# A two-layer encoder on one core: one of two dense blocks finished behind the next layer's first normalisations, with 90 instead of 50 late gather steps

## The chip, the cores and the metric

The kernel runs on one core of a Trainium2 chip. The metric is the time of one execution in microseconds (us) as the device measures it; lower is better. The engines of the core are named as the profile names them: PE (TensorE, matrix products), PEld (its weight loads), DVE (VectorE), ACT (ScalarE), POOL (GpSimd, which also issues the gathers) and SP (SyncE, which issues the ordinary loads). Each engine takes its instructions in the order in which they stand in its queue.

## The reference

The input is 512 tokens of width 1024, with two layers. Each layer mixes tokens and then applies a lookup layer named PEER, each with a residual and a normalisation:

```
h   = LN(x) * (1 + scale1(c)) + shift1(c)
mix = W_o [ MLA(h) | ShortConv(h) | StickBreaking(h) ]
x   = LayerNorm(alpha * x + (1 + gate1(c)) * mix)
h   = LN(x) * (1 + scale2(c)) + shift2(c)
x   = LayerNorm(alpha * x + (1 + gate2(c)) * PEER(h))
```

PEER has 128 x 128 experts, each with one row of a table u and one row of a table v (1024 floats each). A token has 8 heads with 16 chosen experts each, so 128 experts. For each of them the output gets gelu(u_e . h) times the expert's weight times v_e. The choice is made by queries against two sets of 128 keys and two rounds of top-k.

## The kernel before

The 512 tokens are four blocks of 128 (NB = 4), blocks 0 to 3. In a layer every block passes prepare (a normalisation, the tile `ytok`, and its transposes `hT`), project (the input projection, done for blocks 0 and 1 together and for 2 and 3 together), attend, output, between (residual, normalisations, `h2d`), queries and the top-k (topk, which ends with the integer indices `eidx`).

PEER is computed in two ways. Blocks 1 and 2 (DENSE) go through dense(): for each of the 128 key rows the whole rows of u and v are loaded (512 KB each), the scores of all 256 tokens are made (L824 to L826), Gelu (L828), times the gate weights G (L830), and summed into `acc` in PSUM (L854 to L860). G is built in three parts, for rows 0 to 51, 52 to 75 and 76 to 127 (CUTS); the part for rows 52 to 75 is built during rows 0 to 51, the last during rows 52 to 75. Blocks 0 and 3 go through experts(): 256 gather steps a block, each an indirect DMA of one row a token (issued by POOL, L689 for u, L701 for v) into one of four buffers `g`, and one DVE operation on it, a dot (L691) for u or a sum into `acc` (L706) for v, in groups of 32 dots, Gelu (L695) and 32 sums. So a layer has 512 steps.

pace() lays the steps among the rest: EARLY (80 in layer 0, 110 in layer 1) before the dense rows, 32 during the first build, LATE[l] behind the dense rows, and the remaining ones evenly over the 128 rows. A step is tied to a mark: its DVE operation may not come before the marked one. The order on each engine is then made by a scheduler that knows priorities; finish() of a gathered block has a higher priority than all else. In layer 0 the late steps are the last ones of block 3.

finish() adds the gate row, the residual and the last normalisation of a block (L223, L718, L237, L239, L225) and writes `xs[b]`, which the next layer's prepare(b) reads. After the last dense row, dense() copies both blocks' sums from PSUM into two tiles `fa` and finishes both, with tiles from the dense pass's own pools (`dw`, `dps`), which are given back by st.close() afterwards. The mark of the late steps is the finish of block 1. The next layer opens its attention pools, lays the 50 late steps, and goes on with layer_setup (SP's loads of small tables, L287 and on), prepare, layer_keys and project (weights by L151, matmuls L154). Block 3's finish and prepare(3) need all late steps.

Of the kernel before, what the change touches and what calls it, by code (L numbers as in the profile page):

```python
# [11 lines left out]
F32 = mybir.dt.float32  # L12
# [5 lines left out]
OP = mybir.AluOpType  # L18
# [3 lines left out]
P = 128  # L22
D = 1024
# [10 lines left out]
CUTS = (0, 52, 76, 128)  # L34
DENSE = (1, 2)
EARLY = (80, 110)
LATE = (50, 0)
WK = 2
HB = 2
MG = 4  # L40
# [12 lines left out]
def body(ctx, tc, x, c, positions, ada_w, ada_b, w_in, q_norm_g, kv_norm_g, w_uq, w_ukv, conv_w,  # L53
         w_o, ln1_g, ln1_b, peer_wq, peer_k1, peer_k2, peer_u, peer_v, ln2_g, ln2_b, out):
    nc = tc.nc
# [4 lines left out]
    pw = ctx.enter_context(tc.tile_pool(name="pw", bufs=1))  # L60
# [59 lines left out]
    rest = 2 * math.pi  # L120
# [122 lines left out]

    def normalize(dst, src):
        mean, r = moments(src)
        nc.vector.tensor_scalar(dst, src, mean, r, op0=OP.subtract, op1=OP.mult)

    def affine(y, dst, tmp, src, ig, ib, mk=None, pool=None):
        mean, r = moments(src, pool)
# [101 lines left out]
    def prepare(y, b):  # L351
        hT = A.work.tile([P, KT, P], F32, name="hT", bufs=2)
        yt = A.work.tile([P, D], F32, name="ytok", bufs=1)
        normalize(yt, xs[b])
        transpose_cols(hT, yt, KT, scale=y.sc1, bias=y.sh1)
        y.hT[b] = hT

    def project(y, blocks, behind=None):
        l = y.l
# [313 lines left out]
    def experts(y, b, eidx, gw):  # L673
        def after(inst):
            if gate[0] is not None:
                tc.add_manual_dep(inst.ins, gate[0].ins.name,
                                  mybir.DependencyInfo(mybir.DependencyClass.NoSync, mybir.DependencyReason.DATA),
                                  reason="expert sums in pace with the dense tiles")

        h2 = pw.tile([P, D], F32, name="h2")  # L680
        nc.sync.dma_start(h2, h2tok[y.l][b // 2])
        acc = pw.tile([P, D], F32, name="acc")
        dots = pw.tile([P, PH, TOPK], F32, name="dots", bufs=1)
        wts = pw.tile([P, PH, TOPK], F32, name="wts", bufs=1)
        for h0 in range(0, PH, HB):
            slots = [(h, k) for h in range(h0, h0 + HB) for k in range(TOPK)]
            for j, (h, k) in enumerate(slots):
                g = gath.tile([P, D], F32, name="g")
                nc.gpsimd.indirect_dma_start(out=g, out_offset=None, in_=u_flat,  # L689
                                             in_offset=bass.IndirectOffsetOnAxis(ap=eidx[:, h, k:k + 1], axis=0))  # L690
                after(nc.vector.scalar_tensor_tensor(out=g, in0=g, scalar=1.0, in1=h2, op0=OP.mult, op1=OP.mult,  # L691
                                                     accum_out=dots[:, h, k:k + 1]))
                yield
            hs = slice(h0, h0 + HB)
            ge = nc.scalar.activation(wts[:, hs, :], dots[:, hs, :], AF.Gelu)  # L695
            if b == 0 and h0 < 2:
                exp_ln(ge)
            nc.vector.tensor_tensor(wts[:, hs, :], wts[:, hs, :], gw[:, hs, :], op=OP.mult)
            for j, (h, k) in enumerate(slots):
                g = gath.tile([P, D], F32, name="g")  # L700
                nc.gpsimd.indirect_dma_start(out=g, out_offset=None, in_=v_flat,  # L701
                                             in_offset=bass.IndirectOffsetOnAxis(ap=eidx[:, h, k:k + 1], axis=0))
                if h == 0 and k == 0:
                    r = nc.vector.tensor_scalar(acc, g, wts[:, h, k:k + 1], None, op0=OP.mult)
                else:
                    r = nc.vector.scalar_tensor_tensor(out=acc, in0=g, scalar=wts[:, h, k:k + 1], in1=acc,  # L706
                                                       op0=OP.mult, op1=OP.add)
                after(r)
                if h < PH - 1 or k < TOPK - 1:
                    yield  # L710
        tc.cur_priority -= 1000000
        finish(y, b, acc, lambda: psx.tile([P, 512], F32, name="prow", tag="ex"), pw)
        tc.cur_priority += 1000000
        yield
# [9 lines left out]
    def dense(y, blocks, res):  # L724
        l = y.l
# [165 lines left out]
                yield held[0]  # L891
        fas = []
        for i in range(2):
            fa = dw.tile([P, D], F32, name="fa", tag="v", bufs=2)
            for g in range(2):
                nc.scalar.copy(fa[:, g * 512:(g + 1) * 512], acc[i][g])
            fas.append(fa)
        for b, fa in zip(blocks, fas):
            r = finish(y, b, fa, ut, dw)
            if b == min(blocks):  # L900
                held[0] = r
        st.close()
        yield held[0]

    def pace(ex, mark, n):
        gate[0] = mark
        for _ in range(n):
            next(ex)

    ada_first(range(4))  # L910
    for l in range(L):
        if l:
            open_attention(l)
            late()
        y = layer_setup(l)

        def pick(b, v1, fi):
            return topk(l, v1, fi, b, b not in DENSE)

        res = [None] * NB  # L920
        for b in (0, 1):
            prepare(y, b)
        layer_keys(y)
        ps = project(y, (0, 1))
        if l + 1 < L:
            ada_side(0, range(4, 12))
        layer_rows(y)
        behind = None
        for p in ps:
            b = p[0]  # L930
            attend(y, *p)
            if b == 1:
                for b2 in (2, 3):
                    prepare(y, b2)
            h = between(y, b, output(y, b, p[2]))
            r = queries(y, *h, range(4))
            if b == 0:
                behind = r
            res[b] = pick(b, *h[1:])
        p2, p3 = project(y, (2, 3), behind)  # L940
        if l + 1 < L:
            ada_side(1, range(12))
        attend(y, *p2)
        h = between(y, 2, output(y, 2, p2[2]))
        queries(y, *h, range(2))
        attend(y, *p3)
        rt = output(y, 3, p3[2])
        queries(y, *h, range(2, 4))
        res[2] = pick(2, *h[1:])
        h = between(y, 3, rt, lambda: A.ps.tile([P, 512], F32, name="prow", tag="at", bufs=2))  # L950
        queries(y, *h, range(4))
        res[3] = partial(pick, 3, *h[1:])
        A.stack.close()
        dn = dense(y, DENSE, res)
        ex = chain.from_iterable(experts(y, b, *res[b]) for b in range(NB) if b not in DENSE)
        pace(ex, None, EARLY[l])
        groups = 2 * P // TG
        for _ in range(groups):
            mark = next(dn)
            pace(ex, mark, 1)  # L960
        with tc.issue_after(mark.ins):
            res[3] = res[3]()
        n = 2 * 2 * NSLOT - EARLY[l] - LATE[l] - groups
        for a, mark in enumerate(dn):
            if a < NK:
                pace(ex, mark, (a + 1) * n // NK - a * n // NK)
        late = partial(pace, ex, mark, LATE[l])
        if not l + 1 < L:
            late()


_INS = ["x", "c", "positions", "ada_w", "ada_b", "w_in", "q_norm_g", "kv_norm_g", "w_uq", "w_ukv", "conv_w",
# [19 lines left out]
```

## Time and profile before

| | before |
|---|---|
| median of 3 runs | 3501.09 us (3497.18 to 3502.11) |
| profiled execution | 3500.46 us, span 3498.7 us |
| PE busy | 3023.7 us, 86% |
| DVE busy | 2871.1 us, 82% |
| POOL busy | 1443.6 us, 41% |
| ACT busy | 1049.6 us, 30% |
| DMA | 1012.04 MB, mean 289 GB/s |

The program's course, in us from the start of the span: layer 0's attention until about 692, its dense rows until 1741, the boundary of the layers until 1797, layer 1's attention until about 2404, its dense rows until about 3451, and a tail to 3498.7. The busy shares are means over these stages, which have different limits, so each stage is read by itself: by windows (busy time of each engine in a stretch), timelines (instructions in order, in brackets the idle time before one and what ended it) and the chain of work that ended last.

### The profile page before, as it was taken

How to read it: one execution, taken by the hardware profiler on the slowest of the kernel's cores; microseconds unless marked ns; L12 is line 12 of the kernel's file. 1: busy time of each engine (PE TensorE's matmuls, PEld its weight loads, DVE VectorE, ACT ScalarE, POOL GpSimd, SP SyncE). 2: the span in 40 equal slices, each digit the busy share in tenths (PEclk: the TensorE clock that was granted, in tenths of full speed). 3: DMA queues.
4: the chain of work that ended last, by engine and by line, in shares of the span. 5: the costliest groups of instructions: out<-in, count | busy, mean ns of one | idle time of the engine just before them, and what ended most of it. 6: DMA issues, size and time to landing. Idle time of an engine off the chain costs nothing.

```text
span 3498.7 us, 52847 instructions
## 1 busy us (share of the span) xinstructions
PE 3023.7 (86%) x18708; PEld 2088.1 (60%) x18708; DVE 2871.1 (82%) x6385; ACT 1049.6 (30%) x2031; POOL 1443.6 (41%) x1347
## 2 busy tenths in 40 slices
PE   7878878658999999999948888884699999899995
PEld 2333434436777777777624444433477777777774
DVE  3567897999888998777775579889998899987777
ACT  2242433222232333322222323312223323332221
POOL 1034554255444434434451044534444444444434
PEclk9989979859999999999969997896699999999997
DMA  8667978568999888999985587794789998999997
GB/s 290 217 219 240 349 223 301 176 185 268 337 337 345 314 296 307 363 349 343 321 305 196 172 276 270 266 329 157 229 290 358 342 348 312 323 338 349 342 347 242
DMA packets 340057, 1012.04 MB, mean 289 GB/s; under 512 B 40505, under 2 KB 53065, under 8 KB 339793
## 3 DMA queue, kind: packets, MB, share of 16 engines
q0 software_dynamic: 147456, 536.94, 44.0%
q1 hardware_dynamic: 192336, 471.73, 38.5%
q8 instruction: 148, 2.42, 0.3%
q14 instruction: 117, 0.95, 0.1%
HBM read 1002.06 MB, written 6.34 MB: 288 GB/s over the span
## 4 chain that ended last, share of the span: by engine, by line
PE 49%; DVE 23%; DMA 14%; issue 8%; POOL 3%; ACT 2%; SPq 0%; POOLq 0%; DVEq 0%; ACTq 0%
PE acc L860 12%; PE pm L154 7%; PE sp L826 5%; PE sp L824 5%; PE sp L825 5%; PE utp L810 5%; DMA g<-in_peer_u,eidx 4%; DVE g L691 3%; DMA g<-in_peer_v,eidx 3%; DVE acc L706 3%; DMA adw<-in_ada_w 3%; DVE tk_ef L661 2%; DVE o L790 2%; POOL g L689 2%; PE acc L856 2%
## 5 line engine op out<-in xcount | busy, mean ns | idle before, releaser
L701 POOL DMA_INDIRECT g<-in_peer_v,eidx x512 | 616.5, 1204 | 795.9 <-DVE acc L706 522.1
L689 POOL DMA_INDIRECT g<-in_peer_u,eidx x512 | 581.2, 1135 | 740.7 <-DVE g L691 510.1
L706 DVE SCALAR_TENSOR_TENSOR acc<-g,wts,acc 128x1024 f32<-128x1024 f32 x508 | 667.3, 1314 | 73.5 <-DMA g<-in_peer_v,eidx 69.6
L691 DVE SCALAR_TENSOR_TENSOR g<-g,h 128x1024 f32<-128x1024 f32 x512 | 622.8, 1226 | 98.3 <-DMA g<-in_peer_u,eidx 96.2
L824 PE MATMUL sp<-hh,uh 128*128 128x256 f32 x2048 | 622.7, 304 | 12.9 <-ACT ge L828 11.5
L860 PE MATMUL acc<-v,ge 128*128 128x512 f32 x1360 | 619.5, 597 | 7.9 <-DVE ge L830 7.9
L826 PE MATMUL sp<-hh,ul 128*128 128x256 f32 x2048 | 596.3, 291 | 0.4 <-DVE ul L814 0.2
L825 PE MATMUL sp<-hl,uh 128*128 128x256 f32 x2048 | 588.7, 287 | 0.0
L812 ACT CAST uh<-utp 128x512 fp32r<-128x512 f32 x512 | 298.5, 590 | 694.8 <-PE utp L810 559.9
L814 DVE TENSOR_TENSOR ul<-utp,uh 128x512 fp32r<-128x512 f32 x512 | 345.6, 686 | 84.2 <-ACT uh L812 64.0
L824 PEld LDWEIGHTS sp<-hh,uh 128*128 128x128 f32 x2048 | 393.8, 192 | 31.9 <-ACT ge L828 15.9
L825 PEld LDWEIGHTS sp<-hl,uh 128*128 128x128 f32 x2048 | 393.7, 192 | 14.6 <-issue 13.2
L860 PEld LDWEIGHTS acc<-v,ge 128*128 128x128 f32 x1360 | 247.4, 191 | 251.5 <-issue 242.5
L826 PEld LDWEIGHTS sp<-hh,ul 128*128 128x128 f32 x2048 | 393.3, 192 | 0.5 <-DVE ul L814 0.4
L810 PE MATMUL utp<-ident,u 128*128 128x128 f32 x2048 | 304.9, 277 | 13.9 <-DVE ul L814 12.5
L797 PE MATMUL pg<-o,o 128*128 128x52 bf16 (+1 forms) x4608 | 189.7, 192 | 102.5 <-DVE o L790 79.3
L799 ACT COPY G<-pg 128x416 f32<-128x416 f32 (+1 forms) x192 | 146.4, 773 | 433.9 <-PE pg L797 395.8
L810 PEld LDWEIGHTS utp<-ident,u 128*128 128x128 f32 x2048 | 239.4, 142 | 61.7 <-issue 33.7
L797 PEld LDWEIGHTS <-o 128*128 128x128 bf16 x4608 | 164.5, 103 | 157.1 <-issue 79.1
L154 PE MATMUL pm<-wt,hT 128*128 128x512 f32 (+1 forms) x512 | 231.7, 601 | 30.7 <-DMA wt<-in_w_in 18.8
L154 PE MATMUL pm<-wt,h2T 128*128 128x512 f32 x512 | 234.5, 604 | 10.0 <-DMA wt<-in_peer_wq 9.6
L660 POOL TENSOR_TENSOR tk_pick<-tk_hot,tk_ce 128x400 f32<-128x400 bf16 x128 | 121.9, 953 | 145.0 <-DVE tk_hot L658 142.5
(244 smaller groups left out, 4101.2 us busy)
## 6 DMA issues: line engine op xcount, KB each, us to landing
u<-in_peer_u SPq DMA_DIRECT2D x256, 512.0 KB
v<-in_peer_v SPq DMA_DIRECT2D x256, 512.0 KB
wt<-in_peer_wq SPq DMA_DIRECT2D x128, 512.0 KB
adw<-in_ada_w SPq DMA_DIRECT2D x160, 256.0 KB
wt<-in_w_o SPq DMA_DIRECT2D x64, 512.0 KB
wt<-in_w_in SPq DMA_DIRECT2D x48, 512.0 KB
wt<-in_ada_w SPq DMA_DIRECT2D x16, 512.0 KB
g<-in_peer_u,eidx POOLq DMA_INDIRECT x512
```

The lines of the kernel that those rows point to most:

```text
L154: r = nc.tensor.matmul(pm[:, :n], lhsT=lhsT[:, k0 + k, :], rhs=wt[:, k, :n], start=k0 + k == 0, stop=k0 + k == KT - 1)
L689: nc.gpsimd.indirect_dma_start(out=g, out_offset=None, in_=u_flat, in_offset=bass.IndirectOffsetOnAxis(ap=eidx[:, h, k:k + 1], axis=0))
L691: after(nc.vector.scalar_tensor_tensor(out=g, in0=g, scalar=1.0, in1=h2, op0=OP.mult, op1=OP.mult, accum_out=dots[:, h, k:k + 1]))
L701: nc.gpsimd.indirect_dma_start(out=g, out_offset=None, in_=v_flat, in_offset=bass.IndirectOffsetOnAxis(ap=eidx[:, h, k:k + 1], axis=0))
L706: r = nc.vector.scalar_tensor_tensor(out=acc, in0=g, scalar=wts[:, h, k:k + 1], in1=acc, op0=OP.mult, op1=OP.add)
L797: nc.tensor.matmul(pg[:, tt, 0:n], lhsT=o2[:, tt // TI, :, tt % TI], rhs=o1a[:, tt // TI, p, 0:n, tt % TI], start=tt == 0 and p == 0, stop ...
L810: nc.tensor.transpose(pt[:, j * P:(j + 1) * P], u[:, k * P:(k + 1) * P], ident)
L814: nc.vector.tensor_tensor(ul.rearrange("p j t -> p (j t)"), pt, uh.rearrange("p j t -> p (j t)").bitcast(F32), op=OP.subtract)
L824: nc.tensor.matmul(sp, lhsT=uh[:, j, :], rhs=hh[:, k, :], start=k == 0, stop=False)
L825: nc.tensor.matmul(sp, lhsT=uh[:, j, :], rhs=hl[:, k, :], start=False, stop=False)
L826: nc.tensor.matmul(sp, lhsT=ul[:, j, :], rhs=hh[:, k, :], start=False, stop=k == KT - 1)
L860: nc.tensor.matmul(acc[i][g], lhsT=w[:, i * P:(i + 1) * P], rhs=v[:, g * 512:(g + 1) * 512], start=a == 0, stop=a == NK - 1)
```

## The change

After the dense rows only block 1 is finished in the dense pass. Block 2's sums are copied into a buffer of the gather pool (tag "g") instead of the dense pool, and its finish, now with the tile `prow` that the gathered blocks use (one buffer), is put in a list `rest`. In layer 1 it is issued behind prepare(0) and prepare(1); then come the late steps, 90 instead of 50, tied to prepare(1)'s normalisation instead of block 1's finish. The other steps of layer 0 become 310 instead of 350 over the 128 rows. At the end of layer 1, which has no late steps, the finish in `rest` is issued last.

```diff
-LATE = (50, 0)
+LATE = (90, 0)
...
     def normalize(dst, src):
         mean, r = moments(src)
-        nc.vector.tensor_scalar(dst, src, mean, r, op0=OP.subtract, op1=OP.mult)
+        return nc.vector.tensor_scalar(dst, src, mean, r, op0=OP.subtract, op1=OP.mult)
...
-                g = gath.tile([P, D], F32, name="g")
+                g = gath.tile([P, D], F32, name="g", tag="g")
...
-            fa = dw.tile([P, D], F32, name="fa", tag="v", bufs=2)
+            if i:
+                fa = gath.tile([P, D], F32, name="fa", tag="g")
+            else:
+                fa = dw.tile([P, D], F32, name="fa", tag="v", bufs=2)
...
-        for b, fa in zip(blocks, fas):
-            r = finish(y, b, fa, ut, dw)
-            if b == min(blocks):
-                held[0] = r
+        held[0] = finish(y, blocks[0], fas[0], ut, dw)
+        rest.append(lambda: finish(y, blocks[1], fas[1], lambda: psx.tile([P, 512], F32, name="prow", tag="ex"), pw))
         st.close()
         yield held[0]
+
+    rest = []
...
         if l:
             open_attention(l)
-            late()
         y = layer_setup(l)
...
         for b in (0, 1):
-            prepare(y, b)
+            r = prepare(y, b)
+        if l:
+            rest.pop()()
+            pace(ex, r, LATE[l - 1])
         layer_keys(y)
...
-        late = partial(pace, ex, mark, LATE[l])
         if not l + 1 < L:
-            late()
+            pace(ex, mark, LATE[l])
+            rest.pop()()
```

(prepare returns what normalize returns.) Three places show what moves on DVE. A row names the line, the operation, what it writes and reads, and how many stand in a row. `xs_95` to `xs_98` are blocks 0 to 3. The changed file's lines are one higher here (L692 for L691, L707 for L706, L719 for L718).

At the boundary of the layers, before: from block 1's residual to the statistics of block 2's finish.

```order
L718 SCALAR_TENSOR_TENSOR fa<-xs_96,fa 128x1024
L691 SCALAR_TENSOR_TENSOR g,dots<-g,h_10955 128x1024 x2
L237 BN_STATS bnst<-fa 128x6 x2
L239 BN_AGGR bnmv<-bnst 128x2
L225 SCALAR_TENSOR_TENSOR fa<-fa,bnmv,utp 128x512 x2
L225 SCALAR_TENSOR_TENSOR xs_96<-fa,rs_r,utp 128x512 x2
L691 SCALAR_TENSOR_TENSOR g,dots<-g,h_10955 128x1024 x4
L223 TENSOR_TENSOR fa<-fa,utp 128x512 x2
L691 SCALAR_TENSOR_TENSOR g,dots<-g,h_10955 128x1024
L718 SCALAR_TENSOR_TENSOR fa<-xs_97,fa 128x1024
L691 SCALAR_TENSOR_TENSOR g,dots<-g,h_10955 128x1024 x2
```

Now the same place, from the last gate row:

```order
L223 TENSOR_TENSOR fa<-fa,utp 128x512
L223 TENSOR_TENSOR fa<-fa,prow 128x512
L719 SCALAR_TENSOR_TENSOR fa<-xs_96,fa 128x1024
L719 SCALAR_TENSOR_TENSOR fa<-xs_97,fa 128x1024
L237 BN_STATS bnst<-fa 128x6 x4
L239 BN_AGGR bnmv<-bnst 128x2 x2
L225 SCALAR_TENSOR_TENSOR fa<-fa,bnmv,utp 128x512 x2
L225 SCALAR_TENSOR_TENSOR fa<-fa,bnmv,prow 128x512
L225 SCALAR_TENSOR_TENSOR xs_96<-fa,rs_r,utp 128x512 x2
L225 SCALAR_TENSOR_TENSOR fa<-fa,bnmv,prow 128x512
L298 MEMSET sqT 128x1024
```

The dots are gone from between the pieces, and the two finishes go piece by piece in turn.

In layer 1's attention, where block 0's top-k begins, before: the last stick-breaking operation and the first round.

```order
L539 SCALAR_TENSOR_TENSOR sp_18407<-z,sbe 128x512
L610 MAX tk_v<-scs 128x8 x4
L612 MAX_INDEX tk_i<-tk_v,scs 128x8 x4
L615 MATCH_REPLACE scs<-tk_v,scs 128x128 x4
L610 MAX tk_v<-scs 128x8 x4
L612 MAX_INDEX tk_i<-tk_v,scs 128x8 x4
```

Now:

```order
L540 SCALAR_TENSOR_TENSOR sp_18407<-z,sbe 128x512
L707 SCALAR_TENSOR_TENSOR acc<-g,wts,acc 128x1024 x2
L611 MAX tk_v<-scs 128x8 x4
L613 MAX_INDEX tk_i<-tk_v,scs 128x8 x4
L616 MATCH_REPLACE scs<-tk_v,scs 128x128 x3
L707 SCALAR_TENSOR_TENSOR acc<-g,wts,acc 128x1024
L616 MATCH_REPLACE scs<-tk_v,scs 128x128
L611 MAX tk_v<-scs 128x8 x4
L613 MAX_INDEX tk_i<-tk_v,scs 128x8 x4
L707 SCALAR_TENSOR_TENSOR acc<-g,wts,acc 128x1024
```

Sums of the late steps stand between the pieces of the top-k, where there were none.

At the end of the program, before: the rest of block 2's finish among sums, then block 3's (`xs_98`).

```order
L239 BN_AGGR bnmv<-bnst 128x2
L706 SCALAR_TENSOR_TENSOR acc<-g,wts,acc 128x1024
L225 SCALAR_TENSOR_TENSOR fa<-fa,bnmv,utp 128x512 x2
L706 SCALAR_TENSOR_TENSOR acc<-g,wts,acc 128x1024
L225 SCALAR_TENSOR_TENSOR xs_97<-fa,rs_r,utp 128x512 x2
L706 SCALAR_TENSOR_TENSOR acc<-g,wts,acc 128x1024 x2
L223 TENSOR_TENSOR acc<-acc,prow 128x512 x2
L718 SCALAR_TENSOR_TENSOR acc<-xs_98,acc 128x1024
L237 BN_STATS bnst<-acc 128x6 x2
L239 BN_AGGR bnmv<-bnst 128x2
L225 SCALAR_TENSOR_TENSOR acc<-acc,bnmv,prow 128x512 x2
```

Now:

```order
L225 SCALAR_TENSOR_TENSOR xs_96<-fa,rs_r,utp 128x512 x2
L707 SCALAR_TENSOR_TENSOR acc<-g,wts,acc 128x1024 x7
L223 TENSOR_TENSOR acc<-acc,prow 128x512 x2
L719 SCALAR_TENSOR_TENSOR acc<-xs_98,acc 128x1024
L237 BN_STATS bnst<-acc 128x6 x2
L239 BN_AGGR bnmv<-bnst 128x2
L225 SCALAR_TENSOR_TENSOR acc<-acc,bnmv,prow 128x512 x2
L225 SCALAR_TENSOR_TENSOR xs_98<-acc,rs_r,prow 128x512 x2
L223 TENSOR_TENSOR fa<-fa,prow 128x512 x2
L719 SCALAR_TENSOR_TENSOR fa<-xs_97,fa 128x1024
L237 BN_STATS bnst<-fa 128x6 x2
```

Seven sums stand in a row behind block 1's finish; then comes block 3's finish, and block 2's (`xs_97`) behind it.

On ACT the order holds 27 table loads (ACT_TABLE_LOAD) instead of 17. The ten new ones are all in layer 1's attention, around the stick-breaking heads (L536, L537, L549, L551) and the late steps' Gelu (L695).

## Rows read from the trace of the kernel before

**Rows 1.** Windows of dense rows: start:end, length, busy us by engine, PE clock, DMA share, GB/s

```profile
809.60:1178.10 368.50, 357.76 (x2705) 282.36 (x2704) 321.75 (x553) 107.60 (x207) 173.30 (x149) 1.00 0.91 327
1178.10:1381.70 203.60, 196.88 (x1780) 156.14 (x1779) 185.85 (x350) 73.72 (x123) 84.44 (x68) 0.99 0.86 301
1381.70:1733.20 351.50, 350.95 (x2095) 277.12 (x2096) 272.75 (x396) 100.12 (x187) 148.31 (x135) 1.00 0.95 346
...
2885.50:3094.10 208.60, 198.22 (x1766) 157.71 (x1765) 191.62 (x351) 74.03 (x124) 90.95 (x76) 0.98 0.89 314
```

**Rows 2.** The same windows, DVE's dots (L691), then its sums (L706), rows 52 to 75

```profile
1178.10:1381.70 203.60, 38.45 (x64) 0.99 0.86 301
...
1178.10:1381.70 203.60, 39.99 (x32) 0.99 0.86 301
```

**Rows 3.** Timeline of DVE at the boundary: start, us, instruction, idle before it and its releaser

```profile
1748.55 1.23 DVE L691 SCALAR_TENSOR_TENSOR g<-g,h 128x1024 f32<-128x1024 f32 x1 [1.19 <-DMA g<-in_peer_u,eidx]
...
1752.82 1.41 DVE L225 SCALAR_TENSOR_TENSOR xs<-fa,rs_r,utp 128x512 f32<-128x512 f32 x2
...
1774.70 1.23 DVE L691 SCALAR_TENSOR_TENSOR g<-g,h 128x1024 f32<-128x1024 f32 x1 [0.77 <-DMA g<-in_peer_u,eidx]
...
1775.85 1.40 DVE L225 SCALAR_TENSOR_TENSOR xs<-fa,rs_r,utp 128x512 f32<-128x512 f32 x2
...
1794.48 0.81 DVE L246 TENSOR_SCALAR ytok<-xs,bnmv,rs_r 128x1024 f32<-128x1024 f32 x1 [2.18 <-PE pt L258]
1795.21 2.60 DVE L706 SCALAR_TENSOR_TENSOR acc<-g,wts,acc 128x1024 f32<-128x1024 f32 x2
```

**Rows 4.** Timeline of SP's queue at the boundary

```profile
1730.11 0.33 SPq L836 DMA_DIRECT2D v<-in_peer_v  x1
1777.38 0.38 SPq L287 DMA_DIRECT2D sc<-mod  x1
...
1786.71 3.14 SPq L151 DMA_DIRECT2D wt<-in_w_in  x4
```

**Rows 5.** Timeline of PE at the boundary

```profile
1741.07 0.39 PE L856 MATMUL acc<-hi,lo 128*128 128x512 f32 x1
...
1796.85 3.81 PE L154 MATMUL pm<-wt,hT 128*128 128x416 f32 x5 [2.47 <-DMA wt<-in_w_in]
```

**Rows 6.** Windows of layer 1's attention, columns as in rows 1

```profile
1797.00:1870.00 73.00, 66.42 (x191) 31.92 (x192) 42.78 (x78) 18.97 (x52) 30.03 (x28) 0.97 0.93 330
1870.00:1950.00 80.00, 61.22 (x284) 36.84 (x284) 44.13 (x79) 30.55 (x86) 7.77 (x13) 0.89 0.37 122
1950.00:2056.00 106.00, 94.69 (x286) 45.72 (x285) 68.73 (x293) 18.93 (x42) 30.72 (x38) 0.95 0.67 213
...
2130.00:2230.00 100.00, 75.76 (x243) 41.10 (x244) 96.86 (x222) 28.61 (x60) 57.81 (x52) 0.70 0.68 217
```

**Rows 7.** The chain that ended last, layer 1: start, us, what

```profile
1975.16 14.55 PE pm L154 x38
```

**Rows 8.** Timeline of DVE in layer 1: last late sum, prepare(3), first one-hot piece, eidx

```profile
1882.70 1.28 DVE L706 SCALAR_TENSOR_TENSOR acc<-g,wts,acc 128x1024 f32<-128x1024 f32 x1 [3.09 <-DMA g<-in_peer_v,eidx]
...
1941.65 0.81 DVE L246 TENSOR_SCALAR ytok<-xs,bnmv,rs_r 128x1024 f32<-128x1024 f32 x1 [0.76 <-POOL rs_r L230]
...
2010.22 0.87 DVE L661 TENSOR_REDUCE tk_ef<-tk_pick 128x8 f32<-128x400 f32 x1
...
2032.48 0.21 DVE L662 CAST eidx<-tk_ef 128x128 int32<-128x128 f32 x1
```

**Rows 9.** Groups of ACT: line, operation, count, busy us, mean ns, idle before

```profile
L342 ACT ACT_TABLE_LOAD x6 | 7.7, 1283 | 0.1
```

**Rows 10.** Timeline of DVE at the end: first sum, block 3's finish, its last piece

```profile
3449.88 1.28 DVE L706 SCALAR_TENSOR_TENSOR acc<-g,wts,acc 128x1024 f32<-128x1024 f32 x1 [2.33 <-DMA g<-in_peer_v,eidx]
...
3484.74 0.69 DVE L223 TENSOR_TENSOR acc<-acc,prow 128x512 f32<-128x512 f32 x1
...
3494.05 0.75 DVE L225 SCALAR_TENSOR_TENSOR xs<-acc,rs_r,prow 128x512 f32<-128x512 f32 x1 [0.68 <-PE prow L220]
```

More of the change, by code (lines that the diff above doesn't have):

```diff
@@ L353, in prepare @@
         yt = A.work.tile([P, D], F32, name="ytok", bufs=1)
-        normalize(yt, xs[b])
+        r = normalize(yt, xs[b])
         transpose_cols(hT, yt, KT, scale=y.sc1, bias=y.sh1)
         y.hT[b] = hT
+        return r
     def project(y, blocks, behind=None):
@@ L699, in experts @@
             for j, (h, k) in enumerate(slots):
-                g = gath.tile([P, D], F32, name="g")
+                g = gath.tile([P, D], F32, name="g", tag="g")
                 nc.gpsimd.indirect_dma_start(out=g, out_offset=None, in_=v_flat,
```

## The prediction

> **What bounds the kernel now.** I read four stretches, each first by the busy time of the engines in a window, then by the timeline of the engine that waits.
>
> The dense rows of layer 0: in the last 52 of the 128 rows PE is busy 350.95 of 351.5 us, in the first 52 it is 357.76 of 368.5, in the 24 rows between (which also build the next part of G) 196.88 of 203.6 [rows 1]. So PE sets the pace, and in the middle rows VectorE (DVE) takes a little: layer 1's same 24 rows, which carry more gather steps (2.89 a row by the code, 2.73 in layer 0), last 208.6 us, 5.0 longer, and PE is idle 10.4 us in them against 6.7 [rows 1].
>
> The boundary of the layers: the last dense matmul ends at 1741.5 on PE, block 1's finish on DVE at 1754.2, block 2's at 1777.25, with dots between its pieces [rows 3, 5]. SP starts nothing from 1730.4 until 1777.38, 0.13 us after block 2's finish; then it loads layer 1's small tables and the first projection weight [rows 4], and PE gets its first projection matmul at 1796.85 [rows 5]. SP's loads go into memory that the dense pass's pool holds, and that pool is free only when both finishes in it are done. This is a stall with one releaser.
>
> Layer 1's first attention stretch, 1797 to 2056: PE is busy 66.42 of 73, 61.22 of 80 and 94.69 of 106 us, DVE 42.78, 44.13 and 68.73; the DMA share is 0.93, then 0.37 and 0.67. Later, 2130 to 2230, DVE is the full engine, 96.86 of 100 [rows 6]. The 32 late sums of before run from 1795.21 to 1882.70 [rows 3, 8]; then DVE has none until block 0's gathers, which start behind eidx at 2032.48 [rows 8].
>
> The tail: sums and the finishes of blocks 1 and 2 run mixed from 3449.88 to 3484.74, then block 3's finish alone to 3494.8 [rows 10].
>
> **The change part by part.** Sums are made against the profiled execution, 3500.46 us (span 3498.7 and 1.8 around it), which is 0.6 below the median of 3501.09.
>
> *Forty steps leave the dense rows of layer 0.* 350 steps over 128 rows become 310: 0.3125 a row less. In the 24 middle rows that is 7.5 steps of 1.2 to 1.25 us of DVE (38.45 us for 32 dots, which L691's column counts twice for their accumulator reads, and 39.99 for 32 sums) [rows 2], 9.2 us; but PE is idle there only 6.7 us [rows 1], so 6.7 is the cap. In the last 52 rows nothing: 0.55 us of PE idle. In the first 52 PE is idle 10.7 us; layer 1 has more steps in these rows at no visible loss, so I put 1.3 there. Together **-8**, between -4 (half the cap) and -12 (half of the first rows' idle time on top).
>
> *One finish instead of two in front of SP.* In the new order DVE runs the two finishes piece by piece in turn, with no dot between. A finish alone takes 10.1 us (3484.74 to 3494.8) [rows 10]; from 1741.5, with three pieces of the other block in its way, block 1's finish ends near 1754, as before. But SP now waits for that one alone: its loads start near 1754.3 instead of 1777.4, **-23**, and not beyond -25 (an undisturbed finish) nor less than -18 (all of the other finish in its way). Everything behind is pulled along: the second ytok, at 1794.48 [rows 3], comes at about 1772.
>
> *Ninety late steps between ytok and eidx.* Behind ytok, where 32 sums stood, now stand 90 (26 sums, 32 dots, 32 sums): 58 more, and each gathers 128x1024 f32, 0.524 MB. They are laid in DVE's queue between the pieces of block 0's attention, its normalisations and its top-k rounds. DVE goes in order, so a gather that comes late holds the top-k behind it, and eidx (the indices that let layer 1's gathers begin) cannot come before the last of them, then 14 of the 16 one-hot pieces (22.3 us for 16 from 2010.22 to 2032.48 [rows 8], so 19.5), block 3's finish (10.1 [rows 10]) and a normalisation, 33 us together. So eidx = 1772 + 90 x pace + 33.
>
> For the pace there are two rows. Beside weight loads (DMA share 0.93): 32 sums in 88.8 us, 31 intervals, 2.86 us each [rows 3, 8]. Without them, at the boundary, from the dot at 1748.55 to that at 1774.70, both held by their gathers: 12 steps in 26.15 us, 2.18 each [rows 3]. The crowded stretch of before is 73 us long [rows 6]; that much at 2.86 is 26 steps, the other 64 at 2.18 take 140 us. eidx comes at 1772 + 73 + 140 + 33 = 2018, against 2032.5: **-14** (the -23 is in it). All at 2.18 gives 2001, -31; all at 2.86 gives 2062, +30. I take the mixture because the share falls from 0.93 to 0.37 after the first loads [rows 6]. Counter-check by DVE: its 140 us of before (the three windows less the 15 behind eidx) and 58 x 1.25 = 73 are 213 us; from 1774 to 2018 that is 87% of DVE, between the 60% of now and the 97% that rows 6 show to be possible.
>
> The Trainium skill (DMA: Bandwidth & Descriptors, Queues, rings and completion order) says that each DMA engine takes packets in turn from the queues that have work; by it gathers and weights would share the 330 GB/s of that window in halves, 0.524 MB at 165 GB/s or 3.2 us a step. The measured 2.86 agrees roughly. By the rule 23 steps fit into the crowded stretch, the three others cost 7 us behind it, and the whole sum would be -3.
>
> *What is pushed behind eidx.* prepare(3), at 1941.65 before [rows 8], waits for block 3's finish, which now ends just ahead of eidx. So the projection of blocks 2 and 3 moves behind it: 48 matmuls of 512 columns at 0.38 us (14.55 for 38) [rows 7], 18 us if nothing hides them, 0 if PE's idle 24 of 100 us do [rows 6]. And ScalarE's order has ten more table loads (27 instead of 17), since Gelu of late groups now falls between Exp and Ln of the stick-breaking heads: 1.283 us each [rows 9], 12.8 us, on an engine that is busy 29 of 100 us there [rows 6]. Its waiters are stick-breaking weights on DVE and PE. Together 0 to +31; I take **+6**, since both engines have room in the rows. Below zero I exclude it: DVE is full there, and the same operations in another order don't shrink its sum. The Trainium skill (ScalarE: Activation LUTs, What ACT_TABLE_LOAD costs) prices a load at about 2.7 us with its drain; the row says 1.283 and decides. By the page's figure it would be 27 us, and, if the same part of it reached the path, the sum 5 us later.
>
> *The tail.* In layer 1 block 2's finish is issued last. Before, both finishes hid between sums. Now 15 sums with one finish need 32.7 us at 2.18, or 27 if DVE alone sets it (15 x 1.25 and 8 of the finish), against 34.9: 2 to 8 us gained. Then come two finishes in a row: 10.1 more [rows 10]. **+6**, between +2 and +8.
>
> The sum: -8 - 14 + 6 + 6 = **-10**. 3500.46 - 10 is 3490.5; against the median, 3491.
>
> **The rivals.**
>
> *The late chain is slower than the stall it replaces (slower than before).* The first weight loads are only moved, w_o's and the queries' follow, and if the gathers meet loads all the way, 90 steps at 2.86 put eidx at 2062: -8 + 30 + 12 = +34, 3535. It decides from the pace: the sum is zero where eidx comes at 2028.5, a mean of 2.48 us a step; above 2.56 it is a loss that shows. For it: the two means lie 2.18 and 2.86, the middle is 2.52. Against it: DMA share 0.37 in the 80 us behind the first loads.
>
> *No change.* The pace lies between 2.41 and 2.56: the 23 us saved at the boundary are used up by DVE and the gathers before eidx. 3494 to 3508.
>
> *All late steps hide.* 2.18 throughout, and what is pushed back finds idle engines: -8 - 31 + 6 = -33, 3468. For it: DVE idles 40% there now. Against: the weight loads' share of 0.93 in the first 73 us, which they don't lose by coming earlier [rows 6].
>
> *It doesn't do what it says.* If SP's loads were held by something else than block 2's finish (another pool, ordered behind the late steps), the -23 is missing: -10 + 23 = +13, 3513. Against it: 0.13 us between that finish and SP's first load, and in the new order nothing of block 2 is in the dense pass's pool.
>
> **How the numbers follow.** Forecast, 3480 to 3494: 0.36. All hide: 0.10. No change: 0.26. Late chain slower: 0.24, from 3508 up, thinning out toward 3535. Not as it says: 0.04. A measurement of this kernel tells some 0.2%, 7 us, from nothing. So faster 0.46, same 0.26, slower 0.28. The range leaves out the outermost tenth on either side: low, dense -12 with a pace of 2.2 or so, 3472; high, a pace of 2.68 with the other terms as taken, 90 x 0.2 = 18 us above zero change, 3520.
>
> **What would show it.** SP's first load of layer 1 within 2 us of block 1's finish, and the first projection matmul some 23 us earlier after the last dense matmul. The 24 middle rows of layer 0 about 197 us. Late steps at 2.2 to 2.5 us, eidx of block 0 some 277 us after the last dense matmul (before 291). Block 2's finish alone at the end, 10 us. The forecast is wrong if DVE waits for gathers all through layer 1's first top-k, or if layer 1's dense rows begin later than before, counted from the last dense matmul of layer 0.

## The result: 1.4% slower

The changed kernel takes 3551.77 us (median of 4 runs, 3548.5 to 3561.9) where the kernel before took 3501.6 beside it: a ratio of 1.0144, 95% interval 1.0122 to 1.0167. The forecast was 3491, the range ended at 3520, and the sign was wrong.

The head of the profile of the changed kernel: the span, busy time by engine, and two rows of the span in 40 slices (busy tenths of PE, granted clock of PE in tenths).

```profile
span 3553.0 us, 52877 instructions
...
PE 3046.9 (86%) x18708; PEld 2100.7 (59%) x18708; DVE 2875.6 (81%) x6385; ACT 1064.0 (30%) x2041; POOL 1461.7 (41%) x1347
...
PE   7878879659999999999887596685699999899995
...
PEclk9989989859999999999898796897699999999997
```

PE's row before:

```profile
PE   7878878658999999999948888884699999899995
```

The work is the same: as many matmuls and DVE instructions as before, DVE busy 4.5 us more; PE is busy 23.2 us more with the same matmuls (the last section takes that up). What changed is where engines stand idle, and one stage shows it: slices 21 to 27, between the two blocks of dense rows.

The table cuts the profiled executions into stages, by rows that every trace has: the start of the first Gelu of row 0, 52, 76 and 127 in each layer, the end of the last dense matmul, layer 1's first projection matmul, the start of block 0's eidx in layer 1, and the end of the span. Columns are the kernel before, the changed one and six experiments, which follow below (late 50 is the changed kernel with 50 late steps, and so on).

| us | before | changed | late 50 | before, late 90 | tail as before | late 50, tail as before | prepare(3) loose | rows 0 to 75 as before |
|---|---|---|---|---|---|---|---|---|
| to row 0 of layer 0 | 692.3 | 689.0 | 687.9 | 687.0 | 690.1 | 689.5 | 684.3 | 689.5 |
| rows 0 to 51 | 485.8 | 491.3 | 490.2 | 494.1 | 494.9 | 487.8 | 498.2 | 488.0 |
| rows 52 to 75 | 203.6 | 210.2 | 202.6 | 209.5 | 207.8 | 203.2 | 210.6 | 207.7 |
| rows 76 to 127 | 351.5 | 352.3 | 351.8 | 354.0 | 354.5 | 351.5 | 353.3 | 353.3 |
| to the last dense matmul | 8.3 | 6.2 | 9.2 | 6.2 | 8.1 | 8.5 | 6.2 | 5.2 |
| to the first projection | 55.4 | 21.6 | 25.7 | 35.4 | 22.1 | 25.7 | 21.3 | 21.4 |
| to eidx of block 0 | 235.6 | 271.3 | 251.7 | 266.3 | 265.9 | 248.2 | 272.3 | 273.6 |
| to row 0 of layer 1 | 371.6 | 403.0 | 371.5 | 371.2 | 399.6 | 372.1 | 362.3 | 391.6 |
| layer 1's rows and its last dense matmul | 1050.7 | 1058.0 | 1049.0 | 1050.4 | 1055.6 | 1050.5 | 1061.8 | 1053.2 |
| to the end | 43.9 | 50.0 | 53.0 | 44.2 | 41.3 | 43.6 | 49.2 | 49.4 |

Changed against before: the boundary gives 33.8 us, layer 0's rows take 10.9 with their last matmuls, the way to eidx 35.7, from there to layer 1's rows 31.4, layer 1's rows 7.3, the end 6.1, and the start gives 3.3: 54.3 in all.

Each column is one profiled execution, and executions differ with nothing changed. Up to row 0 the instructions of PE, DVE, ACT and POOL stand in the same order in all twelve traces of this document, and the stretch takes 684.3 to 692.3 us. Rows 52 to 75 have the same order in "late 50, tail as before" and "rows 0 to 75 as before", and take 203.2 and 207.7. So a difference of under some 5 to 8 us in one row of the table is not shown by two columns alone.

The stall at the boundary is gone, as SP's timeline of the changed kernel shows beside [rows 4]:

```profile
1739.61 0.33 SPq L837 DMA_DIRECT2D v<-in_peer_v  x1
1759.90 0.38 SPq L287 DMA_DIRECT2D sc<-mod  x1
...
1764.38 2.96 SPq L151 DMA_DIRECT2D wt<-in_w_in  x4
```

and PE's, beside [rows 5]:

```profile
1748.00 1.08 PE L857 MATMUL acc<-hi,lo 128*128 128x512 f32 x4
...
1770.72 3.11 PE L154 MATMUL pm<-wt,hT 128*128 128x416 f32 x4 [1.99 <-DMA wt<-in_w_in]
```

SP's first load starts 0.1 us after block 1's finish (its `xs` ends at 1759.8, in the fence after the next) and 10.8 us behind the last dense matmul, where before it was 35.9.

DVE, beside [rows 3, 8]: the end of block 1's finish, first and last of the 90 late steps, prepare(3) and eidx.

```profile
1758.37 1.40 DVE L225 SCALAR_TENSOR_TENSOR xs<-fa,rs_r,utp 128x512 f32<-128x512 f32 x2
...
1769.56 3.92 DVE L707 SCALAR_TENSOR_TENSOR acc<-g,wts,acc 128x1024 f32<-128x1024 f32 x3
...
2012.34 1.40 DVE L707 SCALAR_TENSOR_TENSOR acc<-g,wts,acc 128x1024 f32<-128x1024 f32 x1
...
2037.98 0.80 DVE L246 TENSOR_SCALAR ytok<-xs,bnmv,rs_r 128x1024 f32<-128x1024 f32 x1
...
2042.00 0.20 DVE L663 CAST eidx<-tk_ef 128x128 int32<-128x128 f32 x1
```

Ninety steps from 1769.6 to 2013.7 are 2.7 us each. prepare(3) stood 200 us behind the last dense matmul before [rows 5, 8]; now it stands 289 us behind it.

Windows of the same stages (columns as in [rows 1]): from the first projection to eidx of block 0, and from eidx of block 1 to the dense rows. First the kernel before.

```profile
1796.90:2032.50 235.60, 207.49 (x717) 107.88 (x718) 140.84 (x424) 66.26 (x172) 54.89 (x62) 0.95 0.64 213
...
2215.40:2404.00 188.60, 137.12 (x600) 75.51 (x598) 166.62 (x553) 48.75 (x86) 77.20 (x77) 0.88 0.77 269
```

The changed kernel:

```profile
1770.70:2042.00 271.30, 197.31 (x655) 102.99 (x656) 211.10 (x516) 72.06 (x172) 120.19 (x122) 0.83 0.79 280
...
2208.80:2445.00 236.20, 172.45 (x725) 93.13 (x723) 187.52 (x580) 67.21 (x117) 88.02 (x85) 0.88 0.73 252
```

In the first row DVE went from 140.84 of 235.6 us to 211.10 of 271.3, about the 58 more steps at 1.25; its mean there is 78%. PE did 62 matmuls fewer in 36 us more. In the last row PE has 125 more to do, in 48 us more.

### The profile page after: what moved, and what is told of

It is laid out like the page before. It is cut to its first block, busy times and chain, and to the rows that moved or that the text cites. A ratio compares the mean times of both kernels' runs of the same rounds, so it can differ in the third digit from the quotient of the medians.

```text
span 3553.0 us, 52877 instructions
## 1 busy us (share of the span) xinstructions
PE 3046.9 (86%) x18708; PEld 2100.7 (59%) x18708; DVE 2875.6 (81%) x6385; ACT 1064.0 (30%) x2041; POOL 1461.7 (41%) x1347
## 4 chain that ended last, share of the span: by engine, by line
PE 49%; DVE 23%; DMA 14%; issue 8%; POOL 3%; ACT 2%; SPq 0%; POOLq 0%; DVEq 0%; ACTq 0%
PE acc L861 11%; PE pm L154 8%; PE sp L825 5%; PE sp L827 5%; PE sp L826 5%; PE utp L811 5%; DMA g<-in_peer_u,eidx 3%; DVE g L692 3%; DMA g<-in_peer_v,eidx 3%; DMA adw<-in_ada_w 3%; DVE acc L707 3%; DVE tk_ef L662 3%; DMA v<-in_peer_v 2%; PE acc L857 2%; PE acc L856 2%
## 5 line engine op out<-in xcount | busy, mean ns | idle before, releaser
L690 POOL DMA_INDIRECT g<-in_peer_u,eidx x512 | 595.3, 1163 | 790.1 <-DVE g L692 522.4
L707 DVE SCALAR_TENSOR_TENSOR acc<-g,wts,acc 128x1024 f32<-128x1024 f32 x508 | 670.9, 1321 | 84.7 <-DMA g<-in_peer_v,eidx 79.6
L692 DVE SCALAR_TENSOR_TENSOR g<-g,h 128x1024 f32<-128x1024 f32 x512 | 620.1, 1223 | 120.5 <-DMA g<-in_peer_u,eidx 117.7
```

## The experiments

Theory 1 was that the late steps cost DVE time wherever they stand; theory 2 that what the change moves costs (block 2's finish, the projection of blocks 2 and 3, table loads), whatever the count. Theory 3, which came out of the first runs, is that the late steps cost by holding prepare(3), on which the way to layer 1's rows hangs. Ratios are against the kernel before on the same chip.

**50 late steps in the changed kernel.**

```diff
-LATE = (90, 0)
+LATE = (50, 0)
```

> The changed kernel with 50 late steps as before (block 2's finish stays behind prepare(1), the other steps go back into layer 0's rows). Theory 1, the late steps themselves cost: between layer 1's first projection and its dense rows the changed kernel lost 67 us with 58 more sums and dots there, 1.16 us each; with 50 late steps only 18 are more than before, so 21 us lost, 34 gained at the boundary, 6 lost at the end: about -7 against before, 3495 us. Theory 2, the moved work costs (block 2's finish and prepare(3) standing elsewhere, the projection of blocks 2 and 3 behind the first top-k, table loads), whatever the count: the 67 us stay, -34 + 67 + 6, about 3540 us.

Measured: 3491.54 us, ratio 0.9973 (0.9957 to 0.9989). That is theory 1's number (its mechanism is taken up under theory 3); theory 2 falls, as stated for any count. The boundary keeps 30 of its 34 us, and the stage behind eidx is 371.5 us, that of before.

**90 late steps in the kernel before.**

```diff
-LATE = (50, 0)
+LATE = (90, 0)
```

> The kernel before with 90 late steps instead of 50 and nothing else changed: both finishes stay in the dense pass and the late steps start at the boundary. Theory 1 (the steps cost): 40 more in layer 1's attention at 1.16 us, +46, and up to 13 more if the 24 middle rows of layer 0 again don't get shorter: 3540 to 3560 us. Theory 2 (the moved work costs): within 10 us of before, 3491 to 3511.

Measured: 3529.96 us, ratio 1.0090 (1.0060 to 1.0119): slower, between the numbers of theory 1 (from 3540) and theory 2 (to 3511). The profiled execution, at 3520.03 us, is the fastest of the five, so the table shows too little of this loss. The count alone moves eidx by 31 us, but 20 come back at the boundary (35.4 instead of 55.4, with both finishes still in SP's way): in DVE's timeline 6 sums stand among the finishes, none waiting for its gather, where 16 dots stood before, four of them waiting, and block 2's finish ends 21 us behind the last dense matmul instead of 36. So the two halves of the change overlap there, and its 33.8 us are not owed to the one finish alone.

**No late steps.**

```diff
-LATE = (90, 0)
+LATE = (0, 0)
```

> The changed kernel with no late steps: all of layer 0's steps stand in its rows (400 over 128 rows, 3.125 a row). Theory 1: no sum or dot in layer 1's attention before eidx, so 32 fewer than before at 1.16, -37, and -34 at the boundary, +6 at the end, and in the rows 50 more steps at 0 to 0.4 us: 3436 to 3456 us. Theory 2: the moved work keeps its 67 us: about 3540. A third, that the rows can't take the steps (1.25 us each in the rows): +62, about 3500.

Measured: 3540.7 us, ratio 1.0118 (1.0081 to 1.0155). That is theory 2's number, but by luck: its 67 us do not stay (eidx comes 221.0 us behind the first projection, row 0 371.1 us behind eidx, together 15 us less than before; theory 1 wants 37 less). The rows took 13.5 us more for 50 more steps (485.6, 208.0 and 360.8 us), and the loss is that the first projection came 90.7 us behind the last dense matmul. The window of that stretch (columns as in [rows 1]):

```profile
1751.00:1842.00 91.00, 4.04 (x18) 2.56 (x18) 63.92 (x80) 7.87 (x10) 55.09 (x54) 0.52 0.82 269
```

PE is idle; DVE works off 41 steps that were laid into the rows and didn't get done there: its last sum of layer 0 starts at 1842.61. What holds PE comes from the change itself. Block 2's sums are now copied into a buffer of the gather pool, which becomes free only behind steps that stand in front of it, and PE's first transposes of layer 1 wait for that copy. ACT and then PE:

```profile
1838.90 1.07 ACT L900 COPY fa<-acc 128x512 f32<-128x512 f32 x2 [59.94 <-DVE acc L707]
```

```profile
1840.03 1.97 PE L258 MATMUL pt<-ident,ytok 128*128 128x128 f32 x8 [71.49 <-ACT fa L900]
```

Why the transposes need the copy the trace does not name; that they share PSUM room with the dense pass's sums is the likely reason, not a shown one.

**Layer 1's two blocks finished as before.**

```diff
-            if i:
+            if i and l + 1 < L:
                 fa = gath.tile([P, D], F32, name="fa", tag="g")
...
-        rest.append(lambda: finish(y, blocks[1], fas[1], lambda: psx.tile([P, 512], F32, name="prow", tag="ex"), pw))
+        if l + 1 < L:
+            rest.append(lambda: finish(y, blocks[1], fas[1], lambda: psx.tile([P, 512], F32, name="prow", tag="ex"), pw))
+        else:
+            finish(y, blocks[1], fas[1], ut, dw)
...
-            rest.pop()()
```

> The changed kernel, but in layer 1 both dense blocks are finished in the dense pass as before; layer 0 as changed. If the 6 us at the end are the price of two finishes in a row: 6 us less than the changed kernel, 3546 us, and 44 us from the last dense matmul to the end instead of 50. If the end is set by the gathers anyway: 3552, no difference.

Measured: 3542.22 us, ratio 1.0119 (1.0085 to 1.0152), and 41.3 us from the last dense matmul to the end instead of 50.0. The interval overlaps that of the changed kernel (1.0122 to 1.0167), so it is the tail in the trace that shows it: the two finishes in a row are the price. DVE at the end of the changed kernel, block 3's finish and block 2's, first and last piece of each:

```profile
3528.14 0.69 DVE L223 TENSOR_TENSOR acc<-acc,prow 128x512 f32<-128x512 f32 x1
...
3537.44 0.75 DVE L225 SCALAR_TENSOR_TENSOR xs<-acc,rs_r,prow 128x512 f32<-128x512 f32 x1 [0.68 <-PE prow L220]
3538.93 0.69 DVE L223 TENSOR_TENSOR fa<-fa,prow 128x512 f32<-128x512 f32 x1 [0.74 <-PE prow L220]
...
3548.31 0.75 DVE L225 SCALAR_TENSOR_TENSOR xs<-fa,rs_r,prow 128x512 f32<-128x512 f32 x1 [0.68 <-PE prow L220]
```

**Theory 3: prepare(3) let loose.** In all these runs the end of the last projection matmul of blocks 2 and 3 and the first Gelu of layer 1's rows lie 323 to 331 us apart (not 329 to 331, as the expectation below has it), while eidx of block 0 lies 41 to 75 us ahead of that matmul. So the path to the rows goes through that projection, which needs prepare(3), and prepare(3) needs block 3's finish and with it every late step. In the kernel before, PE at the start and the end of that projection, and then ACT:

```profile
1981.87 7.84 PE L154 MATMUL pm<-wt,hT 128*128 128x416 f32 x22
...
2071.38 1.88 PE L154 MATMUL pm<-wt,hT 128*128 128x512 f32 x4
```

```profile
2404.03 0.38 ACT L828 ACTIVATE ge<-sp 128x256 f32<-128x256 f32 x1
```

In the changed kernel:

```profile
2041.45 4.76 PE L154 MATMUL pm<-wt,hT 128*128 128x416 f32 x12
...
2114.87 1.88 PE L154 MATMUL pm<-wt,hT 128*128 128x512 f32 x4
```

```profile
2444.99 0.38 ACT L829 ACTIVATE ge<-sp 128x256 f32<-128x256 f32 x1
```

330.8 us and 328.2. The starts tell when prepare(3) holds the projection: in the changed kernel block 3's part begins 3.5 us behind prepare(3)'s normalisation (2037.98), as soon as its transposes are there, while before the projection begins 40 us behind it (1941.65), directly behind matmuls of the queries (`pm<-wt,h2T`, until 1982.0). So it is in the twelve traces: where prepare(3) stands 277 us or more behind the last dense matmul (five of them, all with 90 late steps), the open matmuls follow it in 3.4 to 4.0 us; in the other seven they come 27 to 46 us later. The test lets prepare(3) go:

```diff
-        r = normalize(yt, xs[b])
+        r = normalize(yt, xs[2 if y.l and b == 3 else b])
```

> The changed kernel, but layer 1's prepare(3) normalises block 2's rows in place of block 3's (so its input projection and attention work on block 2's values): it no longer waits for block 3's finish and the late steps; their number and place stay. In every run so far layer 1's dense rows begin 329 to 331 us behind the last matmul of the projection of blocks 2 and 3. Theory 3, the late steps hold the path through prepare(3) and that projection: its last matmul comes 20 us or more earlier, and the dense rows begin 31 us earlier behind eidx, 3520 us. Theory 1, each late step costs DVE time wherever it stands: no change, 3552.

Measured: 3521.11 us, ratio 1.0049 (1.0034 to 1.0065), 31 us below the changed kernel with the same 90 late steps (eidx comes 272.3 us behind the first projection, as with 271.3). PE and ACT in it:

```profile
2071.42 7.06 PE L154 MATMUL pm<-wt,hT 128*128 128x512 f32 x16
```

```profile
2408.50 0.38 ACT L829 ACTIVATE ge<-sp 128x256 f32<-128x256 f32 x1
```

Again 330.0 us apart. The last projection matmul ends 325.9 us behind the last dense matmul (at 1752.6 in this trace) instead of 367.7 in the changed kernel, and the stage behind eidx takes 362.3 us instead of 403.0; layer 0's rows and layer 1's were some 7 and 4 us longer in this profile, so that 31 to 33 are left in the time. Theory 3 stands for what was lost behind eidx; theory 1 doesn't explain it. What is lost ahead of eidx does go with the number of steps: with the tail as before, the way from the first projection to eidx is 229.4, 248.2, 250.1 and 265.9 us with 30, 50, 60 and 90 of them. (ACT has 23 table loads here instead of 27; the next run bears on those.)

**No table switch.** Plain copies for the late group's Gelu and for block 0's first two in layer 1, and there no load of the common table of Exp and Ln (exp_ln) behind them:

```diff
-            ge = nc.scalar.activation(wts[:, hs, :], dots[:, hs, :], AF.Gelu)
+            if (y.l, b, h0) in ((0, 3, PH - HB), (1, 0, 0), (1, 0, HB)):
+                ge = nc.scalar.copy(wts[:, hs, :], dots[:, hs, :])
+            else:
+                ge = nc.scalar.activation(wts[:, hs, :], dots[:, hs, :], AF.Gelu)
-            if b == 0 and h0 < 2:
+            if b == 0 and h0 < 2 and not y.l:
                 exp_ln(ge)
```

> The changed kernel, but the late group's Gelu of block 3 in layer 0 and those of block 0's first two groups in layer 1 are plain copies: ACT's order has 13 table loads instead of 27, none inside the stick-breaking heads. If the table loads are on the path: 14 x 1.283 = 18 us less, 3534. If they run beside other work (theories 1 and 3): 0 to 6 us less, 3546 to 3552.

Measured: 3553.19 us, ratio 1.0149 (1.0123 to 1.0175): no gain that shows. Fourteen table loads of 1.283 us fewer are not worth the 18 us that they would cost on the path (that would be a ratio of 1.009). A few us are neither shown nor excluded: the interval is some 9 us wide to either side.

**50 late steps and the tail as before.** The edits of the first and the fourth run together.

> The changed kernel with 50 late steps, and layer 1's two dense blocks both finished in the dense pass as before. If the two effects seen apart add up (3491.5 with 50 late steps; 9.6 us less where the tail is as before): 3482 us, below the kernel before by 15. If the late steps' number already moved what the tail costs: 3491.

Measured: 3484.93 us, ratio 0.9950 (0.9935 to 0.9966), faster than both kernels. The gains add up, nearly: 25.7 us at the boundary and 43.6 at the end, where the run with 50 late steps alone had 53.0. Their intervals overlap (0.9957 to 0.9989 there), so what the old tail adds is shown by the traces and not by the times.

**30 late steps and the tail as before.**

> As the run with 50 late steps and the tail as before, but 30 late steps (layer 0's rows carry 370 steps, 2.89 a row, as layer 1's do). If each late step costs in layer 1's attention and the rows keep up with 2.89: 20 x 0.8 less, 3466 us. If the gathers fall behind the rows already at 2.89, as they do at 3.125 (the first projection 91 us behind the last dense matmul instead of 26): 3490 to 3520.

Measured: 3487.58 us, ratio 0.9954 (0.9937 to 0.9972), as with 50. Both numbers miss, the second by 2 us. eidx comes 229.4 us behind the first projection instead of 248.2, 19 us less where 16 were expected, but the first projection comes 34.6 us behind the last dense matmul instead of 25.7, with 14 steps still open there, and the rows 52 to 75 take 211.9 us instead of 203.2. So the rows are left behind already at 2.89 steps a row, as the second expectation has it, only less than it says.

**60 late steps and the tail as before.**

> The changed kernel with 60 late steps and the tail as before. With 50 the last late sum ended at 1888 and the second pair of prepare came at 1920, so some ten more steps fit before they hold prepare(3). If only that path counts: the attention as with 50, the first projection 0 to 4 us earlier behind the dense rows, 3481 to 3485. If each step costs its DVE time: 10 x 0.8 more, 3493.

Measured: 3495.46 us, ratio 0.9990 (0.9971 to 1.0010): nearest to the second number, but not by its mechanism. The attention is within 4 us of that with 50 (250.1 and 373.8 us, 23.3 at the boundary), as the path through prepare(3) says. What the profile shows of the loss is in layer 0's rows: 493.3 us for rows 0 to 51 and 207.7 for 52 to 75, with 340 steps instead of 350, and 5 us in layer 1's.

**The steps of rows 0 to 75 as before.** The 40 fewer steps all leave the last 52 rows:

```diff
+        cut = LATE[0] - 50 if l == 0 else 0
+
+        def upto(a):
+            return a * (n + cut) // NK - max(0, a - CUTS[2]) * cut // (NK - CUTS[2])
...
-                pace(ex, mark, (a + 1) * n // NK - a * n // NK)
+                pace(ex, mark, upto(a + 1) - upto(a))
```

> The changed kernel with 90 late steps and 310 steps in layer 0's rows, but rows 0 to 75 keep the steps a row that they have with 350, and the last 52 rows carry the 40 fewer. If fewer steps a row are what made layer 0's rows 0 to 51 longer by 4 to 9 us and rows 52 to 75 by 4 to 7 (the order in which DVE's queue then mixes steps, G's building and the rows' own operations): rows 0 to 51 486 to 490 us, rows 52 to 75 203, the last 52 still 351 to 353, in all about 12 us less than the changed kernel, 3540. If another part of the change did it: 3552 and 210 in the 24 rows.

Measured: 3531.94 us, ratio 1.0082 (1.0055 to 1.0109), 20 us below the changed kernel, more than expected. But the rows gave only 5.8 of it (488.0 and 207.7, not 203); 11 came behind eidx, where the order is another once more. So the expectation holds for rows 0 to 51. The 24 rows decide nothing: "late 50, tail as before" has their instructions in the same order and took 203.2 us.

What can be read from the 24 rows is a wait that fewer steps leave behind. DVE's waits in them, the kernel before and then the changed one (us in total, times, longest):

```profile
DVE o L781 <- PE pg L797: 5.2, 4, 1.9
```

```profile
DVE o L782 <- PE pg L798: 17.3, 13, 1.9
```

PE's longest waits there, before and then changed:

```profile
PE pg L797 <- DVE ul L814: 4.7, 4, 2.1
```

```profile
PE pg L798 <- DVE ul L815: 6.3, 4, 2.7
PE sp L825 <- ACT ge L829: 4.1, 4, 1.2
```

The window of the changed kernel for these rows, beside the second of [rows 1]:

```profile
1180.30:1390.60 210.30, 198.91 (x1781) 157.52 (x1779) 176.65 (x341) 73.20 (x124) 71.98 (x60) 0.98 0.79 271
```

With nine steps fewer (55 for 64) DVE has 9.2 us less to do there (176.65 us for 185.85) and waits 12 us longer for PE's products of G's building. PE and DVE hand G's pieces back and forth, and a step that is gone leaves a wait: 14.1 to 17.3 us in the five traces with 310 steps spread as in the change, 2.4 to 5.2 in the four with the steps of before. Why the stretch gets longer and not just no shorter stays open: the steps of before gave 202.6 to 207.7 us in those four, 310 gave 207.8 to 211.4 in the five, 340, 370 and 400 gave 207.7, 211.9 and 208.0.

## Why the prediction was wrong, point by point

**Forty steps leave the rows: forecast -8, measured +10.9.** The failed step is "PE sets the pace, and in the middle rows DVE takes a little". DVE's busy share and layer 1's longer stretch were read as a price for each step. A wait in a ring of two engines was taken for a full engine: of PE's 6.7 us of idle time there 4.7 are waits of G's products for DVE, and they don't go with the steps: with 9.2 us of steps less PE is idle 11.4 us. The first 52 rows, put at 1.3 us less, took 5.5 more. What makes the rows longer stays open. Only the claim on the last 52 rows (nothing) was right.

**One finish in front of SP: forecast -23, measured -33.8.** The mechanism was right: SP's first load comes 25.1 us earlier, the end of the range that was given. The rest was not in the sum: from SP's first load to the first projection matmul it is 10.8 us instead of 19.5. Beside these loads POOL issues one gather instead of seven, and the DMA share is 0.74 instead of 0.96; that this is the reason is likely and not tested. Before, and then changed:

```profile
1777.30:1796.90 19.60, 1.99 (x9) 1.65 (x9) 14.35 (x25) 8.62 (x12) 14.82 (x20) 0.50 0.96 291
```

```profile
1759.80:1770.70 10.90, 3.70 (x14) 2.19 (x14) 8.11 (x14) 7.86 (x10) 6.89 (x14) 0.50 0.74 171
```

**The pace of the late steps: forecast 2.38 us on average, measured 2.7.** The step that failed is "the other 64 at 2.18". 2.18 was read as the gathers' pace beside no weight loads, but DVE was 89% busy there, with dots and finishes. And the share of 0.37 behind the first loads [rows 6], on which the mixture rests, was read where hardly a late step was left: the sums end at 1882.70 [rows 8]. With 90 steps the share stays at 0.88. The stretch where 2.18 was measured, and that of the 90 steps:

```profile
1748.50:1774.70 26.20, 4.68 (x16) 1.88 (x15) 23.37 (x40) 0.00 (x0) 16.44 (x17) 0.50 0.72 235
```

```profile
1769.60:2013.70 244.10, 189.46 (x626) 98.42 (x627) 183.90 (x468) 71.16 (x169) 106.00 (x103) 0.87 0.88 313
```

Of these 244.1 us DVE spends 113 on steps, 71 on other work between them and 60 waiting, 28.5 of the 60 for gathers and the rest for PE, ACT and other loads. So the steps neither run at 2.18 nor fill DVE. Whether the loaded DMA or DVE's other work and waits set the 2.7 is not separated by any run. From the last dense matmul to eidx it is 292.9 us; forecast 276.5, before 291.0.

**What is pushed behind eidx: forecast +6, measured +31.4.** This is the largest miss, and it is one of choice. The bound went to 31; 6 was taken because "both engines have room in the rows". The projection was priced as 18 us of PE work that might hide. Its size was wrong too: the sum has 48 matmuls, the trace 128 (96 of 512 columns, 32 of 416), 55 us busy, and in the changed kernel 112 of them stand behind prepare(3), from 2041.45 to 2116.75. And it is not work beside the path, it is the path: layer 1's rows begin 323 to 334 us behind its end in all twelve traces, and prepare(3) had moved from 200 to 289 us behind the last dense matmul. The run with prepare(3) loose shows it; the one without table switches rules out that the loads cost their full time on ACT. The Trainium skill (ScalarE: Activation LUTs, What ACT_TABLE_LOAD costs) prices a switch at about 2.7 us with its drain, by which the ten loads would have cost still more; no run here shows a cost of theirs. (By the prediction's own proportion that figure makes the sum 3 us later, not 5.)

**The tail: forecast +6, measured +6.1**, and the run with the old tail took 8.7 out. The mechanism and the size were right.

**Not in the sum:** layer 1's rows, 7.3 us longer, and the start, 3.3 shorter. The start does the same in the same order, so that much comes from the executions alone; for layer 1's rows no run tells the change from that.

**The signs.** Of the two signs of being wrong that the prediction named, the second came: layer 1's dense rows begin 695.9 us behind the last dense matmul of layer 0 instead of 662.5.

**The rivals.** Nearest to what came is the first, the late chain that is slower than the stall it replaces. Its point of decision, a mean pace above 2.56, was right, and the pace was 2.7. But its loss was to come by a late eidx, and eidx came only 1.9 us later than before behind the last dense matmul; at a pace of 2.7 its sum gives some 20 us of the 54, since it too priced the way behind eidx at 6 and took 8 off for the rows. The chance of 0.24 rested on the free pace of the boundary.

## What to carry to other kernels

Work that is moved out of a stall and tied in front of a step that others need costs by the way it holds, not by its busy time: look for the row that stands at a constant distance from the end of the stage, and ask what the moved work does to that row. A share of idle time in a queue that goes in order is not yet room for work; take the pace from a stretch with the same neighbours: the 2.86 measured in the attention was nearer to the 2.7 that came than the 2.18 of the boundary. Of a change with two halves, try each alone before both: here the late finish with 50 late steps is worth 0.3%, and with the old tail 0.5%.

## What was not expected

PE's granted clock: from the first projection to eidx of block 0 it is 0.83 in the changed kernel and 0.95 before, with PE busy 197.31 of 271.3 us instead of 207.49 of 235.6. Matmuls of one kind are dearer there: `pm<-wt,cat` 0.692 us each instead of 0.625 (64 in both), `prow<-rows,sel` 0.352 (48) instead of 0.288 (40). That the slower stretch, in which PE stands idle more, makes its own work slower fits this; no run tests it.

Layer 0's rows 0 to 51 take longer with fewer steps: 485.6 to 490.2 us in the six traces with 171 or 172 steps in them, 491.3 to 498.2 in the six with 155 to 168. The ranges do not meet, though the same order of instructions can differ by 5 us (498.2 and 493.2, prepare(3) loose and no table switch). What a step that is gone costs there stays open.
